# A dilated attention stage: permutation in smaller pieces, output weights loaded ahead of their split, one merge placed later

## The chip, the core and the metric

The kernel runs on one core of a Trainium2 chip. A core has a matrix engine (TensorE, in the profile PE, with its weight loads as PEld), a vector engine (VectorE, DVE), an activation engine (ScalarE, ACT), a general engine (GpSimd, POOL) and a queue engine that mostly issues transfers (SyncE, SP). Each takes its instructions in a fixed order and waits on semaphores for the others. The metric is the device time of one execution in microseconds, as the median over runs.

## The reference

Two encoder layers over 1024 tokens of width 1024. Layer 0 mixes tokens with latent attention, layer 1 with dilated windows; each ends with a squared-ReLU MLP. The change touches layer 1's mixer alone. What it must compute, shortened:

```python
DIL_GROUPS = ((128, 1), (512, 4), (2048, 16))      # window, dilation

def dilated_mixer(h, pos, w_in, g_q, g_k, rel_bias, w_o):
    proj = (h @ w_in).reshape(B, S, 3, 3, 16, 64)
    for gi, (window, dilation) in enumerate(DIL_GROUPS):
        q = rms_norm(proj[:, :, gi, 0], g_q[gi])
        k = rms_norm(proj[:, :, gi, 1], g_k[gi])
        v = proj[:, :, gi, 2]
        o, lse = dilated_group(q, k, v, pos, table, window, dilation)
        ...
    wts = jax.nn.softmax(jnp.stack(lses, axis=0), axis=0)
    o = jnp.einsum('gbsh,gbshd->bshd', wts, o_all)
    return o.reshape(B, S, 1024) @ w_o
```

So three groups of 16 heads attend, each over tokens taken at stride 1, 4 or 16, and their outputs are merged with weights from the three softmax denominators before the output projection.

## The kernel before

**Form of the numbers.** The program first runs a variant in which a matrix is a pair of 16-bit floats (a high and a low part), so that a product is three matmuls (`mm3`, L530 to L534). A second variant of the same code (`half` false) stands behind a branch, and the execution profiled here does not enter it. To split a loaded f32 weight into its pair takes one ACT instruction (L156, the high part) and one on DVE (L161, the low part).

**Order of the work.** The Python code gives an order, and a scheduler then moves instructions on each engine as far as their dependences allow; for PE the order of this stage is fixed as the code has it (`pin_from`). So where a step of the code lands on ACT, DVE, POOL and SP is seen in the built program.

**The dilated stage** is `dil` (L2194). It walks 96 steps `("qk", g, pr, tp)`: three groups g, eight pairs of heads pr, four blocks tp of 256 tokens; six steps without a projection follow. In one step the kernel

- scores two units of tokens of an earlier step on PE (`pss`, L2386), takes maxima and sums on DVE (`pd`, L2407, into `stat`), exponentiates on ACT (L2411, L2413), splits the result (`ph`, ACT L2450, DVE or POOL L2451) and transposes it with a DMA that SP issues (`pT`, L2452); in the last group's last pair PE transposes instead (`pspt`, L2439);
- projects 256 tokens to q and k on PE (`psproj`, L532 to L534, in two halves `project(..., 0, ...)` and `project(..., 1, ...)`);
- between those halves transposes q and k of an earlier step on PE (`psq`, L2354) and splits them into `kT` (ACT L2359, DVE L2360); the next scores read `kT`;
- multiplies by v on PE (`psav`, L2466 to L2468), which DVE copies to `U` (L2472, L2475);
- normalises the new q and k: squares on ACT (`dsq`, L2333), sum on DVE (`dms`, L2334), inverse root on ACT and DVE (`drl`, `dry`, `drt`: L132 to L136), product on DVE (`qn`, L2343) and gain on POOL or DVE (L2345).

Weights of q and k come pair by pair: `wqkr` is loaded by SP (L1968) and split to `wqk` (L156, L161).

**The permutation.** Groups 1 and 2 need the tokens in another order. `permute(g, dp, k)` (L2655 to L2684) copies one quarter of the channels of one part into new tiles `hTp` of the shared pool `G`; a call makes 4 copies of 128x512 for group 1 (`hTp<-hT` and `hTp<-hs`) and 8 of 128x256 for group 2 (`hTp<-hTp`). Copies go round by number over ACT (L2680), DVE (L2682) and POOL (L2684), two, two and one of five. There are eight calls before each new group: one at step (7, 2) of the old group, two at (7, 3), and five in `both` (L2232), which is the first projection of the new group, taken channel quarter by channel quarter. That first step is called the turn here.

**The merge.** `factors` (L2542 to L2558) makes the weights `mgf` of the three groups; `merge` (L2560 to L2569) multiplies group 2's `U` on DVE and the other groups' tiles `um` on POOL (L2567), and adds on DVE (L2569). It is called at a pair's last unit (`finish`). `emit` (L2576) transposes the merged pair on PE (`psot`, L2586) and splits it into `oT`, stored to memory for pairs 0 to 5 and kept for 6 and 7.

**The end of the stage.** `tail` (L2901) is called in the four last steps. It loads a quarter of the output weights (`wo_raw`, L1374, tile `wor`, L538 on SP) in the first and second of them, splits one (`wo_form`, tile `wo`) in the third and fourth, and in the fourth also loads and splits the other two (`wo_load`). Then `proj_res` (L1389) forms the output projection `psy`.

Of the kernel before, what the change touches and what calls it, by code (L numbers as in the profile page):

```python
# [15 lines left out]
ALU = mybir.AluOpType  # L16
# [4 lines left out]
P = 128  # L21
# [20 lines left out]
class K:  # L42
# [2151 lines left out]
    def dil(self, at0, at1, tail, wqk, vd, back=None):  # L2194
# [305 lines left out]
        O = [[[None] * 4 for _ in range(2)] for _ in range(2)]  # L2500
        merged = []

        def finish(u):
# [22 lines left out]
            if pr == 0:  # L2526
                sums_back(1)
            if pr < 7:
                f = factors(pr, 0, 8)
                for hf in range(2):  # L2530
                    merge(u, hf, f[:, :, 4 * hf : 4 * hf + 4])
                merged.append((u, u["at"], (0, 1)))
            else:
                last(u, 1)
# [41 lines left out]
        def emit(u, ths):  # L2576

            pr = u["pr"]
            if pr == 6:
                for k in range(2):  # L2580
                    for th in range(2):
                        O[k][th][3] = self.G(f"oT{k}", (P, 2, 512), self.DT)
# [72 lines left out]
        def permute(g, dp, k):  # L2655

            for th in range(2):
                if not self.half:
                    x = self.G("hTp", (P, 2, 512))
                elif k == 0:  # L2660
                    x = self.pair(self.G, "hTp", (P, 2, 512))
                    new_lo[(dp, th)] = x[1]
                    x = x[0]
                else:
                    x = new_lo.pop((dp, th))
# [30 lines left out]
        for n, step in enumerate(steps):  # L2696
            for f in vtodo.pop(n, ()):
                f()
            turn = step is not None and step[2:] == (0, 0) and bool(perms)
            if step is not None and step[1] < 2 and step[2] == 7 and step[3] >= 2:  # L2700
                if step[3] == 2:
# [15 lines left out]
            transposed, scored = scored, attend(ready, n > end) if ready else []  # L2717
            fetch(n)
            for u_, t_, _ in scored:
                if u_["g"] == 2:  # L2720
# [48 lines left out]
            if step is not None:  # L2769
                stacking = (u, tp, qkstep(u, tp, ps))  # L2770
                if n == end:
                    self.pin_from(mark, mybir.EngineType.PE)
# [3 lines left out]
                    if not self.half:  # L2776
                        for pp in range(3):
                            self.reload(O, src, pp, 0, nc.sync)
            if self.half and n == end + 1:
                back()  # L2780
# [19 lines left out]
def run(tc, a, half):  # L2800
    nc = tc.nc
    with ExitStack() as ctx:
# [97 lines left out]

        def tail(tp):  # L2901
            if tp < 2:
                raws.append(k.wo_raw(a["dil_w_o"][0], 0, tp))
# [76 lines left out]
```

## Time and profile before

| | us |
|---|---|
| median of 3 runs | 2974.12 (2973.5 to 2976.3) |
| the profiled execution, its own time | 2971.93 |
| its span, first to last instruction | 2970.1 |
| PE busy in the span | 2813.5 |
| DVE busy | 2237.1 |
| ACT busy | 1687.8 |

The mean granted clock of PE is 0.981. The dilated stage lies from about 1537 to 2275 us of the span, a step every 7.1 us; the turn to group 1 is near 1744 us, that to group 2 near 1982 us. A row of a timeline has the start, the duration, the engine, the line, the operation, the tiles written and read, the number of instructions, and in brackets how long the engine had been idle before and what released it. `x10` behind a row are ten instructions in a run. "Busy" of PE includes time at a lower clock.

### The profile page before, as it was taken

How to read it: one execution, taken by the hardware profiler on the slowest of the kernel's cores; microseconds unless marked ns; L12 is line 12 of the kernel's file. 1: busy time of each engine (PE TensorE's matmuls, PEld its weight loads, DVE VectorE, ACT ScalarE, POOL GpSimd, SP SyncE). 2: the span in 40 equal slices, each digit the busy share in tenths (PEclk: the TensorE clock that was granted, in tenths of full speed). 3: DMA queues.
4: the chain of work that ended last, by engine and by line, in shares of the span. 5: the costliest groups of instructions: out<-in, count | busy, mean ns of one | idle time of the engine just before them, and what ended most of it. 6: DMA issues, size and time to landing. Idle time of an engine off the chain costs nothing. (4 is left out here: it accounts for less than half of the span.)

```text
span 2970.1 us, 55695 instructions
## 1 busy us (share of the span) xinstructions
PE 2813.5 (95%) x20788; PEld 1678.5 (57%) x20788; DVE 2237.1 (75%) x4827; ACT 1687.8 (57%) x3491; POOL 924.9 (31%) x1272
## 2 busy tenths in 40 slices
PE   6888999999999999999999999998997999999998
PEld 5644566644444444443468888877875544444443
DVE  5687777648988866689757877777786698779565
ACT  4677888826455533452228878776664355555331
POOL 5578888700111000001113334445562001110010
PEclk9999999999999999999999999999998999999999
DMA  6267555424755689555635656756677555447753
GB/s 210 65 172 157 109 105 115 126 78 157 244 205 185 233 248 317 186 188 189 222 111 145 150 140 155 167 136 139 138 134 177 161 205 199 159 177 249 243 192 86
DMA packets 589684, 503.15 MB, mean 169 GB/s; under 512 B 292277, under 2 KB 482018, under 8 KB 589402
## 3 DMA queue, kind: packets, MB, share of 16 engines
q1 hardware_dynamic: 553722, 400.74, 48.9%
q0 software_dynamic: 25248, 87.22, 7.9%
q10 hardware_dynamic: 10432, 11.54, 1.7%
q8 instruction: 164, 2.69, 0.4%
q14 instruction: 118, 0.97, 0.1%
HBM read 317.40 MB, written 125.12 MB: 149 GB/s over the span
## 5 line engine op out<-in xcount | busy, mean ns | idle before, releaser
L532 PE MATMUL psm<-hf,wf 128*128 128x512 f16 x896 | 341.2, 381 | 5.1 <-ACT wf L156 5.1
L533 PE MATMUL psm<-d,d 128*128 128x512 f16 x896 | 340.4, 380 | 4.7 <-DVE d L161 4.7
L534 PE MATMUL psm<-hf,wf 128*128 128x512 f16 x896 | 335.0, 380 | 6.4 <-DVE wf L161 6.3
L533 PE MATMUL psm<-hf,wf 128*128 128x512 f16 x896 | 340.9, 380 | 0.0
L534 PE MATMUL psm<-d,d 128*128 128x512 f16 x896 | 340.4, 380 | 0.0
L532 PE MATMUL psm<-d,d 128*128 128x512 f16 x896 | 334.7, 380 | 0.3 <-ACT d L156 0.3
L1276 POOL TENSOR_TENSOR pp<-p,pp 128x1024 f16<-128x1024 f32 x125 | 275.5, 2209 | 57.9 <-ACT pp L1269 46.1
L532 PE MATMUL psproj<-wqk,hTp 128*128 128x256 f16 x1024 | 284.0, 277 | 0.0
L533 PE MATMUL psproj<-wqk,hTp 128*128 128x256 f16 x1024 | 283.5, 277 | 0.0
L534 PE MATMUL psproj<-wqk,hTp 128*128 128x256 f16 x1024 | 283.2, 277 | 0.0
L156 ACT ACTIVATE d<-ufr 128x1024 f16<-128x1024 f32 x112 | 117.8, 1052 | 211.9 <-PE psm L534 170.7
L897 DVE TENSOR_REDUCE mx<-pmx 128x1 f32<-128x512 f32 x240 | 162.9, 687 | 78.9 <-PE pmx L895 77.6
L161 DVE SCALAR_TENSOR_TENSOR d<-ufr,d 128x1024 f16<-128x1024 f32 x112 | 136.5, 1218 | 74.8 <-ACT d L156 74.7
L1268 ACT ACTIVATE p<-pss 128x512 f32<-128x512 f32 x256 | 150.1, 591 | 43.1 <-PE pss L1259 41.7
L2413 ACT ACTIVATE pd<-pd,dnb 128x192 f32<-128x192 f32 (+2 forms) x384 | 167.6, 438 | 2.6 <-ACT dnb L2411 0.4
L534 PEld LDWEIGHTS <-wf 128*128 128x128 f16 x896 | 87.8, 98 | 117.3 <-DVE wf L161 12.9
L532 PEld LDWEIGHTS <-wf 128*128 128x128 f16 x896 | 87.9, 98 | 112.7 <-ACT wf L156 9.6
L534 PEld LDWEIGHTS <-d 128*128 128x128 f16 x896 | 87.8, 98 | 110.8 <-issue 6.1
L271 DVE SCALAR_TENSOR_TENSOR adacc<-adaw,cond,adacc 128x1024 f32<-128x1024 f32 (+1 forms) x98 | 129.0, 1317 | 27.6 <-DMA adaw<-in_ada_w 26.7
L2451 POOL TENSOR_TENSOR ph<-pd,ph 128x512 f16<-128x512 f32 (+1 forms) x121 | 116.9, 970 | 104.0 <-ACT ph L2450 103.3
L532 PEld LDWEIGHTS <-d 128*128 128x128 f16 x896 | 87.9, 98 | 106.2 <-issue 2.0
L533 PEld LDWEIGHTS <-d 128*128 128x128 f16 x896 | 87.9, 98 | 106.1 <-issue 2.0
(445 smaller groups left out, 8176.9 us busy)
## 6 DMA issues: line engine op xcount, KB each, us to landing
ufr<-uf SPq DMA_DIRECT2D x112, 512.0 KB
w2r<-in_mlp_w SPq DMA_DIRECT2D x96, 512.0 KB
adaw<-in_ada_w SPq DMA_DIRECT2D x80, 512.0 KB
w1r<-in_mlp_w SPq DMA_DIRECT2D x64, 512.0 KB
wqkr<-in_dil_w_in SPq DMA_DIRECT2D x96, 256.0 KB
wvr<-in_dil_w_in SPq DMA_DIRECT2D x34, 512.0 KB
uf<-ub POOLq DMA_DIRECT2D x32, 512.0 KB, 3.7
uf<-ua POOLq DMA_DIRECT2D x32, 512.0 KB, 3.4
```

What stands on the lines that cost most here:

```text
L156: nc.scalar.activation(hi, src, AF.Copy, scale=scale)
L161: return nc.vector.scalar_tensor_tensor(lo, src, scale, hi, op0=ALU.mult, op1=ALU.subtract, accum_out=self.seen[:, self.nseen - 1 : self.n ...
L271: return self.nc.vector.scalar_tensor_tensor(acc, w, c, acc, op0=ALU.mult, op1=ALU.add)
L532: mm(out, lh, rh, start=first, stop=False)
L533: mm(out, lh, rl, start=False, stop=False)
L534: mm(out, ll, rh, start=False, stop=last)
L897: nc.vector.tensor_reduce(maxes[h][:, 2 * j + b : 2 * j + b + 1], ps, op=ALU.max, axis=AX.X)
L1268: nc.scalar.activation(p[:, b * 512 : (b + 1) * 512], ps[b], AF.Exp, scale=1.0 / self.ss)
L1276: eng.tensor_tensor(q[:, 1], p, q[:, 0], op=ALU.subtract)
L2413: nc.scalar.activation(p[:, e, lo:hi], p[:, e, lo:hi], AF.Exp, scale=1.0 / self.ss, bias=nb[:, e : e + 1], accum_out=stat[:, g, t, 1, 2 * ...
L2451: (nc.gpsimd if i or u["g"] == 2 else nc.vector).tensor_tensor(lo, p, hi, op=ALU.subtract)
```

## The change

Three things change, all of them in the variant with 16-bit pairs. In the code's order:

1. `permute` is called once in each of six steps, from (6, 2) on to (7, 3) of the old group, and the last two calls stay in `both`. Four of group 1's new tile pairs come from the stage's own pool rather than from `G`.
2. `tail` loads a quarter of the output weights in each of the last four steps and splits it two steps later; the last two splits fall behind the last projection.
3. The merge of pair 6, the last but one, is cut into pieces: `own` (U times its weight, DVE), `other` (a tile `um` times its weight, POOL), `add` (DVE) and `done`, spread over the three steps behind the last projection. It is emitted with the last pair.

```diff
+            if self.half and pr in (6,):
+                f = factors(pr, 0, 8)
...
+                if pr == 6:
+                    at, plan = end + 1, [[(other, 0, 1), (own, 0), (own, 1), (other, 0, 0)],
+                                         [(add, 0, 1), (add, 0, 0), (done, 0), (other, 1, 1), (other, 1, 0)],
+                                         [(add, 1, 1), (add, 1, 0), (done, 1)]]
...
-            if pr == 6:
+            if pr >= 6 and O[0][0][3] is None:
...
-                    x = self.pair(self.G, "hTp", (P, 2, 512))
+                    x = self.pair((lambda name, shape, dt: D_(f"h{dp}{th}", shape, dt, 1)) if g == 1 and dp < 2 else self.G, "hTp", (P, 2, 512))
...
-            turn = step is not None and step[2:] == (0, 0) and bool(perms)
-            if step is not None and step[1] < 2 and step[2] == 7 and step[3] >= 2:
+            turn = step is not None and step[1] > 0 and step[2:] == (0, 0)
+            if self.half and step is not None and step[1] < 2 and (step[2], step[3]) >= (6, 2):
+                if step[2:] == (6, 2):
+                    new = [[[], []], [[], []]]
+                    perms = [(step[1] + 1, dp, k) for dp in range(4) for k in range(2)]
+                for _ in range(1):
+                    if perms:
+                        permute(*perms.pop(0))
...
+            for f, *x in spread.pop(n, ()):
+                f(*x)
...
+            if self.half and n in (end + 1, end + 2):
+                tail(3 + n - end)
...
         def tail(tp):
+            if half:
+                if tp < 4:
+                    raws.append(k.wo_raw(a["dil_w_o"][0], 0, tp))
+                if tp > 1:
+                    wo[0].append(k.wo_form(raws.pop(0)))
+                return
```

In the changed kernel the copies of `permute` are L2708 (ACT), L2710 (DVE) and L2712 (POOL), `own` is L2533, `other` L2537, `add` L2541, the merge's weights L2579 to L2585.

**Where the scheduler puts it.** Of group 1's 32 copies, 16 (names `h_31...`, 7 on ACT, 6 on DVE, 3 on POOL) now stand at the very start of the dilated stage, ahead of its first square, and 16 stay at the turn. Of group 2's 64, 32 (13 on ACT, 13 on DVE, 6 on POOL) stand in one bunch, four to five steps ahead of the other 32, which stay at the turn. Two splits of `wqk` stand in that bunch too. The place of the bunch on DVE, in pair 6 of group 1, before: `kT_23608` is what the scores of the next unit wait for.

```order
L134 SCALAR_TENSOR_TENSOR drt_24328<-dms_24323,dry_24326 128x8
L135 SCALAR_TENSOR_TENSOR drt_24328<-drt_24328,dry_24326 128x8
L136 SCALAR_TENSOR_TENSOR dry_24326<-drt_24328,dry_24326 128x8
L2343 TENSOR_TENSOR qn_24338<-psproj_24237,dry_24326 128x512
L2451 TENSOR_TENSOR ph_24358<-pd_24360,ph_24358 128x512
L2360 SCALAR_TENSOR_TENSOR kT_23608<-psq_24408,kT_23608 128x2x256
```

And after; five more copies (`hTp_24487` and `hTp_24492`) stand in the rows just ahead of these, between L134 and L136.

```order
L2343 TENSOR_TENSOR qn_24338<-psproj_24237,dry_24326 128x512
L2710 COPY hTp_24790<-h_3163_20078 128x2x128
L2710 COPY hTp_24790<-h_3164_20081 128x2x128
L2710 COPY hTp_24795<-h_3163_20078 128x2x128
L2710 COPY hTp_24790<-h_3163_20078 128x2x128
L2710 COPY hTp_24790<-h_3164_20081 128x2x128
L2710 COPY hTp_24795<-h_3163_20078 128x2x128
L2710 COPY hTp_24795<-h_3164_20081 128x2x128
L161 SCALAR_TENSOR_TENSOR wqk_24497,seen_14494<-wqkr_24089,wqk_24497 128x1024
L2472 COPY U_23609<-psav_24439 128x256
L2451 TENSOR_TENSOR ph_24358<-pd_24360,ph_24358 128x512
L2360 SCALAR_TENSOR_TENSOR kT_23608<-psq_24408,kT_23608 128x2x256
```

Twelve copies, with one more a little ahead, and the split of a weight now stand before the `kT` of this step, which stood two rows behind `qn` before.

On ACT, at the end of the stage, in the third and fourth of the last steps; `wo` is a quarter of the output weights being split, `wor` its load. Before:

```order
L156 ACTIVATE wo_29917<-wor_29655 128x1024
L2411 ACTIVATE dnb_29709<-stat,ln_16275 128x2
L2413 ACTIVATE pd_29706,stat<-pd_29706,dnb_29709 128x128 x2
L2411 ACTIVATE dnb_29718<-stat,ln_16275 128x2
L132 ACTIVATE drl_29676<-dms_29672,misc 128x8
L156 ACTIVATE wo_29922<-wor_29920 128x1024
L2450 ACTIVATE ph_29704<-pd_29706 128x256
L2413 ACTIVATE pd_29715,stat<-pd_29715,dnb_29718 128x128 x2
L133 ACTIVATE dry_29675<-drl_29676 128x8
L2359 ACTIVATE kT_29416<-psq_29756 128x2x256
L2553 ACTIVATE mgf_29946<-mgf_29946 128x48
L2450 ACTIVATE ph_29704<-pd_29715 128x256
```

After:

```order
L156 ACTIVATE wo_29921<-wor_29655 128x1024
L2411 ACTIVATE dnb_29709<-stat,ln_16275 128x2
L2413 ACTIVATE pd_29706,stat<-pd_29706,dnb_29709 128x128 x2
L2411 ACTIVATE dnb_29718<-stat,ln_16275 128x2
L132 ACTIVATE drl_29676<-dms_29672,misc 128x8
L2450 ACTIVATE ph_29704<-pd_29706 128x256
L2413 ACTIVATE pd_29715,stat<-pd_29715,dnb_29718 128x128 x2
L133 ACTIVATE dry_29675<-drl_29676 128x8
L2359 ACTIVATE kT_29416<-psq_29756 128x2x256
L2581 ACTIVATE mgf_29940<-mgf_29940 128x48
L2450 ACTIVATE ph_29704<-pd_29715 128x256
L2333 ACTIVATE dsq_29806<-psproj_29731 128x512
```

The split of the third quarter, `wo_29922`, is gone from between the weights of the inverse root and `kT`; the fourth's, which came next after these rows before, is gone too. Both, on DVE as well, come behind the last but one `kT` of the stage or later.

On DVE, the last steps of the projection: the last `qn` (L2343, the last row) is what the last transposes and scores wait for; `um` are the other groups' tiles of pair 6. Before:

```order
L136 SCALAR_TENSOR_TENSOR dry_29808<-drt_29810,dry_29808 128x8
L2567 TENSOR_TENSOR U_28859<-U_28859,mgf_29946 128x512
L2343 TENSOR_TENSOR qn_29820<-psproj_29731,dry_29808 128x512
L2334 TENSOR_REDUCE dms_29966<-dsq_29965 128x8
L2569 TENSOR_TENSOR U_28859<-U_28859,um_29728 128x512
L2345 TENSOR_TENSOR qn_29820<-qn_29820,dgain 128x2x128
L2569 TENSOR_TENSOR U_28859<-U_28859,um_29728 128x512
L134 SCALAR_TENSOR_TENSOR drt_29971<-dms_29966,dry_29969 128x8
L135 SCALAR_TENSOR_TENSOR drt_29971<-drt_29971,dry_29969 128x8
L136 SCALAR_TENSOR_TENSOR dry_29969<-drt_29971,dry_29969 128x8
L2343 TENSOR_TENSOR qn_29981<-psproj_29861,dry_29969 128x512
```

After:

```order
L2334 TENSOR_REDUCE dms_29950<-dsq_29949 128x8
L2533 TENSOR_TENSOR U_28859<-U_28859,mgf_29940 128x512
L2541 TENSOR_TENSOR U_28859<-U_28859,um_29728 128x512
L134 SCALAR_TENSOR_TENSOR drt_29955<-dms_29950,dry_29953 128x8
L2541 TENSOR_TENSOR U_28859<-U_28859,um_29728 128x512
L135 SCALAR_TENSOR_TENSOR drt_29955<-drt_29955,dry_29953 128x8
L136 SCALAR_TENSOR_TENSOR dry_29953<-drt_29955,dry_29953 128x8
L2343 TENSOR_TENSOR qn_29965<-psproj_29863,dry_29953 128x512
```

All four adds of pair 6 still stand ahead of the last `qn`; the multiplication of the second half by its weight (L2567 before, L2533 now) does too, now behind the last `dms`. On POOL the four multiplications of `um` stay together, at the same place. On PE pair 6's eight transposes `psot` move from before the first `psy` to after its first products. On SP three loads of output weights, rather than two, stand ahead of the transposing DMA `pT_29579`, and none behind it.

More of the change, by code (lines that the diff above doesn't have):

```diff
@@ L2500, in dil @@
         O = [[[None] * 4 for _ in range(2)] for _ in range(2)]
-        merged = []
+        merged, spread, now = [], {}, [0]
         def finish(u):
@@ L2527, in finish, with own, other, add @@
                 sums_back(1)
-            if pr < 7:
+            if self.half and pr in (6,):
+                f = factors(pr, 0, 8)
+                def own(hf):
+                    U4 = u["U"][:, 4 * hf : 4 * hf + 4, :].rearrange("p t (h e) -> p t h e", h=2)
+                    nc.vector.tensor_tensor(U4, U4, f[:, 2, 4 * hf : 4 * hf + 4].unsqueeze(3).broadcast_to([P, 4, 2, 64]), op=ALU.mult)
+                def other(hf, k):
+                    x4 = u["um"][hf][:, :, k].rearrange("p t (h e) -> p t h e", h=2)
+                    nc.gpsimd.tensor_tensor(x4, x4, f[:, k, 4 * hf : 4 * hf + 4].unsqueeze(3).broadcast_to([P, 4, 2, 64]), op=ALU.mult)
+                def add(hf, k):
+                    U = u["U"][:, 4 * hf : 4 * hf + 4, :]
+                    nc.vector.tensor_tensor(U, U, u["um"][hf][:, :, k], op=ALU.add)
+                def done(hf):
+                    merged.append((u, now[0], (hf,)))
+                if pr == 6:
+                    at, plan = end + 1, [[(other, 0, 1), (own, 0), (own, 1), (other, 0, 0)],
+                                         [(add, 0, 1), (add, 0, 0), (done, 0), (other, 1, 1), (other, 1, 0)],
+                                         [(add, 1, 1), (add, 1, 0), (done, 1)]]
+                else:
+                    at, plan = now[0], [[(other, 0, 1), (own, 0)], [(other, 0, 0), (add, 0, 1)],
+                                        [(other, 1, 1), (add, 0, 0), (own, 1), (done, 0)],
+                                        [(other, 1, 0), (add, 1, 1)], [(add, 1, 0), (done, 1)]]
+                for i, fs in enumerate(plan):
+                    spread.setdefault(at + i, []).extend(fs)
+            elif pr < 7:
                 f = factors(pr, 0, 8)
@@ L2698, in dil @@
                 f()
-            turn = step is not None and step[2:] == (0, 0) and bool(perms)
-            if step is not None and step[1] < 2 and step[2] == 7 and step[3] >= 2:
+            turn = step is not None and step[1] > 0 and step[2:] == (0, 0)
[6 more added lines that the diff above has]
+                        permute(*perms.pop(0))
+            elif not self.half and step is not None and step[1] < 2 and step[2] == 7 and step[3] >= 2:
                 if step[3] == 2:
@@ L2718, in dil @@
             fetch(n)
+            now[0] = n
             for u_, t_, _ in scored:
@@ L2770, in dil @@
                 stacking = (u, tp, qkstep(u, tp, ps))
+            for f, *x in spread.pop(n, ()):
+                f(*x)
+            if step is not None:
                 if n == end:
```

## The prediction

> **What bounds the kernel now.** I read the page first, then PE's waits in the dilated stage, then the timelines around the places that the change touches.
>
> ```profile
> PE 2813.5 (95%) x20788; PEld 1678.5 (57%) x20788; DVE 2237.1 (75%) x4827; ACT 1687.8 (57%) x3491; POOL 924.9 (31%) x1272
> ```
>
> PE is busy 95% of the span, and the change alters none of its products. It can pay only where PE stands idle or runs at a lower clock. PE's waits from 1540 to 2320 us (us in total, times, longest):
>
> ```profile
> PE pss L2386 <- DVE kT L2360: 19.9, 13, 5.8
> PE psav L2466 <- DMA pT<-ph: 10.7, 6, 2.6
> PE pss L2386 <- DVE qn L2343: 7.1, 1, 7.1
> ```
>
> These are 37.7 us in all, of which the change reaches three places: the two turns and the stage's end. The waits of group 2 in between belong to merges of earlier pairs, which stay as they are.
>
> Turn 2 on PE's timeline, and in windows of 5 us (PE, PEld, DVE, ACT and POOL busy, then PE's granted clock):
>
> ```profile
> 1982.68 0.26 PE L2386 MATMUL pss<-kT 64*128 64x192 f16 x2 [1.17 <-ACT kT L2359]
> 1988.77 0.50 PE L2386 MATMUL pss<-kT 64*128 64x192 f16 x4 [5.83 <-DVE kT L2360]
> ...
> 1980.00:1985.00 5.00, 1.77 (x37) 1.30 (x34) 5.00 (x10) 5.00 (x14) 4.18 (x8) 1.00 1.12 221
> 1985.00:1990.00 5.00, 1.23 (x8) 0.72 (x9) 4.70 (x19) 4.70 (x13) 1.04 (x4) 0.54 0.59 124
> 1990.00:1995.00 5.00, 5.00 (x38) 4.12 (x36) 2.79 (x10) 2.82 (x11) 0.00 (x0) 0.78 0.34 77
> ```
>
> PE stands 1.17 + 5.83 = 7.0 us here. Then the granted clock is 0.54 and 0.78 where it is 1.00 elsewhere: in the last window PE works 5.00 us and 0.22 of that is lost, 1.1 us; with the 1.23 us worked at about half clock just before, some 0.6 more, the half-clock stretch costs 1.7 us.
>
> **Turn 1** (one term). Its waits on PE:
>
> ```profile
> 1745.01 0.61 PE L2386 MATMUL pss<-kT 64*128 64x256 f16 x8 [0.82 <-DVE kT L2360]
> 1752.78 0.20 PE L2466 MATMUL psav<-vs,pT 128*128 128x64 f16 x1 [1.37 <-DMA pT<-ph]
> 1754.46 0.34 PE L2386 MATMUL pss<-kT 64*128 64x192 f16 x4 [0.38 <-DVE kT L2360]
> 1758.73 0.44 PE L2354 MATMUL psq<-ident,qn 128*128 128x128 f32 x2 [1.20 <-DVE qn L2343]
> ```
>
> They sum to 3.8 us. The order puts 16 of the 32 copies at the start of the stage: 7 on ACT, 6 on DVE, 3 on POOL. What hides them there:
>
> ```profile
> 1539.52 0.60 ACT L2333 ACTIVATE dsq<-psproj 128x512 f32<-128x512 f32 x1 [34.62 <-PE psproj L534]
> 1541.67 0.36 DVE L2209 SCALAR_TENSOR_TENSOR dgain<-dgain,dgk 128x192 f32<-128x192 f32 x1 [4.86 <-DMA dgk<-in_dil_g_k]
> ...
> L2680 ACT ACTIVATE hTp<-hT x10: 639/662/674, 1736.5 to 1750.3; 128x512 f16<-128x512 f16 x10
> L2682 DVE COPY hTp<-hT x10: 410/460/906, 1737.7 to 1749.9; 128x512 f16<-128x512 f16 x10
> ```
>
> ACT needs 7 x 0.66 = 4.6 us of an idle 34.62; DVE 6 x 0.46 = 2.8 of 4.86; POOL's three stand ahead of one of its stores of v, which is read a step or more later. I cost them at nothing; without that cover DVE's 2.8 us would be the price. At the turn DVE keeps 7 of 13 copies. The waits on DVE there, 0.82 + 0.38 + 1.20 = 2.4, mostly go; the transposing DMA's 1.37 has its own chain and stays. I take **-2.2**, between 0 (the 7 copies left still come before a `kT`) and -3.8 (all of it).
>
> **Turn 2 and the new bunch** (two terms). The DVE copies of group 2, and how they lie at the turn:
>
> ```profile
> L2682 DVE COPY hTp<-hTp x25: 273/484/1231, 1976.7 to 1988.8; 128x256 f16<-128x256 f16 x25
> ...
> 1977.50 5.06 DVE L2682 COPY hTp<-hTp 128x256 f16<-128x256 f16 x12
> 1982.48 1.21 DVE L161 SCALAR_TENSOR_TENSOR wqk<-wqkr,wqk 128x1024 f16<-128x1024 f32 x1
> 1983.63 3.55 DVE L2682 COPY hTp<-hTp 128x256 f16<-128x256 f16 x10
> 1988.04 0.67 DVE L2360 SCALAR_TENSOR_TENSOR kT<-psq,kT 128x512 f16<-128x512 f32 x1
> ```
>
> The runs of 12 and 10 take (5.06 + 3.55) / 22 = 0.39 us a copy. 23 copies stood ahead of that `kT`. Now 12 do: 11 x 0.39 = 4.3 us earlier, so PE's 7.0 shrinks to 2.7. Whether the half-clock stretch (1.7) then goes is open; I take half of it, 0.8. Turn 2 gives **-5.1** (bounds -4.3, and -8.7 for all of it).
>
> The other 13 DVE copies, `U` and the split of a weight come ahead of a `kT` in pair 6. That place before:
>
> ```profile
> 1950.60 0.69 DVE L2451 TENSOR_TENSOR ph<-pd,ph 128x512 f16<-128x512 f32 x1 [1.43 <-ACT ph L2450]
> 1951.21 0.68 DVE L2360 SCALAR_TENSOR_TENSOR kT<-psq,kT 128x512 f16<-128x512 f32 x1
> 1952.76 0.67 PE L2386 MATMUL pss<-kT 64*128 64x192 f16 x12
> 1953.47 0.41 DVE L2472 COPY U<-psav 128x256 f32<-128x256 f32 x1
> ```
>
> `kT` ends at 1951.89 and the scores begin at 1952.76: the chain has 0.87 us to spare, and DVE idled 1.43 before. Added ahead of `kT`: 13 x 0.39, the split's 1.15 (1983.63 - 1982.48) and 0.41, together 6.6 us, less 1.43 and 0.87: PE stands 4.3 us. Counted from turn 2 instead, which is left with one copy less and already had `U` there, it is 2.7 + 0.39 + 0.41 = 3.5. I take 4.0 and, as before, half of a half-clock stretch: **+4.8**. The lower bound is 2.8, with copies at the shortest 0.273; the upper 4.8 + 1.7 = 6.5, with copies at the 5.06 / 12 = 0.42 of the run that POOL's copies stand beside.
>
> A gain is excluded, since nothing is taken away there. The `qn` behind the bunch is not late: PE takes it a step (7.1 us) later.
>
> What the clock does is seen at two places: the stretch behind the 5.83 us above, and this one at the end of the stage, where PE works 3.89 us at a granted 0.50, some 1.9 lost, though the longest of the waits ahead of it (quoted next) is 2.56:
>
> ```profile
> 2250.00:2255.00 5.00, 3.89 (x26) 2.60 (x27) 4.93 (x18) 2.36 (x6) 1.51 (x5) 0.50 0.54 57
> ```
>
> By that row a wait of 2.7 at turn 2 and one of 4.0 in the bunch may each bring a stretch: turn 2 -4.3, bunch +5.7. The Trainium skill ("TensorE: Matmul & The Clock Gate", HAM oscillation) allows idle gaps of up to about 3.4 us without a fall of the clock. By that rule turn 2 would be -6.0 and the bunch +5.7, and the sum below -6.7 rather than the -5.0 that the row gives; the row at 2250 speaks against the rule. My halves lie between what the two say of each place.
>
> **The end of the stage** (one term). On PE, and what it waits for:
>
> ```profile
> 2248.39 0.23 PE L2466 MATMUL psav<-vs,pT 128*128 128x64 f16 x1 [2.56 <-DMA pT<-ph]
> 2250.25 0.29 PE L2386 MATMUL pss<-kT 64*128 64x128 f16 x2 [1.04 <-ACT kT L2359]
> 2251.40 0.72 PE L2386 MATMUL pss<-kT 64*128 64x128 f16 x10 [0.86 <-DVE kT L2360]
> 2266.93 0.82 PE L2386 MATMUL pss<-kT 64*128 64x128 f16 x11 [7.06 <-DVE qn L2343]
> 2274.80 0.38 PE L2386 MATMUL pss<-kT 64*128 64x128 f16 x4 [1.32 <-DVE oT L161]
> ...
> 2247.48 1.06 ACT L156 ACTIVATE wo<-wor 128x1024 f16<-128x1024 f32 x1 [4.17 <-DMA wor<-in_dil_w_o]
> 2252.68 1.21 DVE L161 SCALAR_TENSOR_TENSOR wo<-wor,wo 128x1024 f16<-128x1024 f32 x1
> 2255.87 0.21 DVE L2557 TENSOR_TENSOR mgf<-mgf,mgd 128x48 f32<-128x48 f32 x1
> 2256.16 5.53 POOL L2567 TENSOR_TENSOR um<-um,mgf 128x512 f32<-128x512 f32 x4 [4.07 <-DVE mgf L2557]
> 2266.18 0.69 DVE L2343 TENSOR_TENSOR qn<-psproj,dry 128x512 f32<-128x512 f32 x1
> ```
>
> ACT waits 4.17 us for a load that it has to split, and `kT` and `ph` queue behind it. With the splits moved back, ACT's `kT` is ready when `psav` ends, so the waits of 1.04 and 0.86 go. DVE loses two splits of 1.21 ahead of `mgf`, and `mgf` comes at about 2252.2 instead of 2255.87: 1.04 + 0.86 earlier scores, plus the second split and part of the first. POOL's 5.53 us of `um` begin with it. The four adds still stand ahead of the last `qn`, so the last `qn` keeps hanging on POOL's `um`: it moves 3.7 us, not the whole 7.06. Behind it the 1.32 for `oT` goes, as pair 6's transposes stand later; they covered a wait for the last `kT` (a pass on ACT and one on DVE, each about the 0.67 of the DVE row above, 1.3, of which I leave 0.5 covered by the products that stay), so 0.8 comes back. Their own time is moved, not saved. The two late splits lie beside `psy`, on engines that wait there. Sum: -3.7 - 1.3 + 0.8 = **-4.2**; bounds -7 (the low clock of 2250 to 2255 goes as well, 1.9, and the 0.8 doesn't come) and 0 (something else holds the last `qn`).
>
> **Sum:** -2.2 - 5.1 + 4.8 - 4.2 = -6.7. The profiled execution took 2971.93 us (span 2970.1 and 1.8 around it), so 2965.2. It lies 2.2 below the median of the runs shown; against that, 2967.4, say **2967**.
>
> **Rivals.**
>
> *More goes than I count* (2960.5): turn 1 -3.4, turn 2 -6.0 with no slow clock left, bunch +2.8, end -7: -13.6. For it speaks that turn 1's waits of up to 1.37 are followed by none; against it that `kT` has only 0.87 us to spare. Chance 0.30.
>
> *Not what it says* (2972.7): the permutation isn't spread over six steps but falls in bunches, as the order shows, so group 2's wait is only moved. Turn 1 -0.6, turn 2 -4.3, bunch +6.5, end -3: -1.4. Chance 0.16.
>
> *Slower, by a load in SP's queue.* SP issues in order, and a third load of weights now stands ahead of the transposing DMA whose `psav` waited 2.56 us:
>
> ```profile
> 2232.38 6.96 SPq L538 DMA_DIRECT2D wor<-in_dil_w_o x2
> 2241.76 1.24 SPq L2452 DMA_TRANSPOSE pT<-ph  x1
> 2238.98 8.48 DMA wor<-in_dil_w_o
> ```
>
> SP was free at 2239.34, 2.4 us before it issued that transposition. If the third load must wait for the landing of one before it, up to 6.96 + 8.48 = 15.4 us, `pT` comes 13.0 late; 3.7 of that is won back behind it. Turns -2.5, end +9.3, clock +1.7: +8.5, 2982.6. It ends slower from a wait of about 12.8 us; below 2.4 it costs nothing. Against it: the loads go to buffers of their own, and the first two were issued in 6.96 together. Chance 0.12.
>
> **Numbers.** The forecast's own case has 0.42, from 2963 to 2971; about a third of it (0.14) lies within 0.2% of 2974.12 (2968.2 to 2980.1, about what a measurement of this kernel can tell from no change). So faster 0.30 + 0.28 = 0.58, same 0.16 + 0.14 = 0.30, slower 0.12. The range reaches from 2956, below the gain of the first rival, to 2978; what lies beyond is most of the slower case and the edge of the first.
>
> **What would show it.** Right: sixteen copies before 1540 with no new wait on PE; a wait of 3 to 4 us for `kT` near 1953, and one of about 2.7 near 1982 where 7.0 stood; ACT's wait for `wor` gone near 2247; the wait for the last `qn` at 5 us or so, with POOL's `um` beginning near 2252. Wrong: no wait near 1953; a wait of `psav` above 2.56 near 2246 with SP held at a `wor`; the last `qn` no earlier against the last projection than now.

## The result, and the profile after

The changed kernel is slower: 2984.1 us in the median of seven executions (2978.99 to 2989.28) against 2976.12 for the kernel before (eight, 2973.5 to 2980.55). The ratio is 1.0028, 95% interval 1.0018 to 1.0037, so +8.3 us (5.4 to 11.0). One further execution, 4743.98 us at a mean granted clock of 0.614, was disturbed and is left out. The forecast was 2967 (2956 to 2978), a gain of 7. The profiled execution after took 2982.83 us (span 2981.0), 10.9 more than the one before.

The page's first line shows that the work is the same; only its time differs.

```profile
PE 2819.1 (95%) x20788; PEld 1678.9 (56%) x20788; DVE 2239.3 (75%) x4827; ACT 1686.9 (57%) x3491; POOL 922.2 (31%) x1272
```

PE's waits from 1540 to 2330 us, after (us in total, times, longest):

```profile
PE pss L2386 <- DVE kT L2360: 17.2, 16, 3.4
PE psav L2466 <- DMA pT<-ph: 13.3, 7, 5.3
PE psot L2614 <- DVE U L2597: 6.6, 3, 3.8
PE pss L2386 <- ACT kT L2359: 5.0, 3, 3.0
PE pss L2386 <- DVE qn L2343: 4.4, 1, 4.4
```

The waits on DVE's `kT` and on its `qn` have shrunk by 2.7 us in total each, as meant. What stands against that are ACT's `kT` (one wait of 3.0) and the transposing DMA (longest 5.3 for 2.6). `psot` has one wait more than before, of 2.6 us near 2306.

**Where the time went.** PE issues 20,788 products in both kernels, nearly all in the same order, so the start of the product of the same number in both traces gives the delay at each point of the program. What each stretch adds to the delay (us; place in the time of before; the last four columns belong to the experiments):

```
stretch                         forecast   after |  e1 perm.  e2 weights  e3 merge  e4 early half
turn 1         1722 to 1766       -2.2     -1.5  |   -1.5       -0.1        0.0      +0.6
               1766 to 1940                +1.1  |   +0.4       +0.8       +2.1      +0.6
new bunch      1940 to 1974       +4.8     +4.5  |   +4.9        0.0        0.0      +3.0
turn 2         1974 to 2006       -5.1     -1.0  |   -0.5       +0.2       +1.3      -0.7
               2006 to 2221                +1.1  |   -1.2       +0.7       +1.6      +1.2
               2221 to 2245                -1.7  |   -1.7       -1.7       -0.1       0.0
end of stage   2245 to 2335       -4.2     +4.3  |   +0.3       -0.2       +3.2      -3.7
behind it      2335 to 2959                +0.4  |    0.0        0.0       +0.4      +3.7
```

From 1722 us on this is +7.2 for the changed kernel. Of the other 3.7 us between the two profiled executions, 3.3 arose ahead of the stage, in code that no edit touches, and 0.4 behind PE's last product. The other kernels below lie between -1.6 and +4.8 ahead of the stage, so this is the spread of single executions. The rows between the named places come and go with a stretch of half clock near 1790 and one near 2225, and e4's +0.6 at turn 1 holds a stretch from 1756.7 to 1760.2; the last section shows why.

**Turn 2.** On PE's timeline, and in windows of 5 us (PE, PEld, DVE, ACT and POOL busy, PE's granted clock):

```profile
1991.99 0.26 PE L2386 MATMUL pss<-kT 64*128 64x192 f16 x2 [2.96 <-ACT kT L2359]
1995.01 0.50 PE L2386 MATMUL pss<-kT 64*128 64x192 f16 x4 [2.77 <-DVE kT L2360]
...
1990.00:1995.00 5.00, 0.26 (x2) 0.10 (x2) 4.99 (x12) 4.96 (x12) 3.26 (x5) 0.73 0.98 193
1995.00:2000.00 5.00, 4.99 (x30) 3.56 (x31) 3.91 (x15) 4.12 (x17) 1.33 (x4) 0.59 0.48 110
```

PE stands 2.96 + 2.77 = 5.7 us where it stood 7.0, and the half clock behind it is still there. The wait on DVE fell from 5.83 to 2.77, very near the 2.7 that the forecast gave, but the wait on ACT just ahead of it grew from 1.17 to 2.96. Before and after, on DVE and ACT, from the timelines of the turn; first before:

```profile
1974.11 0.69 DVE L2334 TENSOR_REDUCE dms<-dsq 128x8 f32<-128x512 f32 x1 [1.03 <-ACT dsq L2333]
1974.84 0.30 ACT L132 ACTIVATE drl<-dms,misc 128x8 f32<-128x8 f32 x1 [0.82 <-DVE dms L2334]
1978.29 1.08 ACT L2680 ACTIVATE hTp<-hTp 128x256 f16<-128x256 f16 x3
```

and after:

```profile
1980.50 0.69 DVE L2451 TENSOR_TENSOR ph<-pd,ph 128x512 f16<-128x512 f32 x1 [2.23 <-ACT ph L2450]
1984.17 0.68 DVE L2334 TENSOR_REDUCE dms<-dsq 128x8 f32<-128x512 f32 x1
1984.88 0.30 ACT L132 ACTIVATE drl<-dms,misc 128x8 f32<-128x8 f32 x1 [2.83 <-DVE dms L2334]
1987.07 2.57 DVE L2710 COPY hTp<-hTp 128x256 f16<-128x256 f16 x6
1987.94 1.09 ACT L2708 ACTIVATE hTp<-hTp 128x256 f16<-128x256 f16 x3
1991.30 1.50 DVE L2710 COPY hTp<-hTp 128x256 f16<-128x256 f16 x6
```

DVE's twelve copies take 4.07 us for the 8.61 of 22, so the saving was counted rightly: 4.5 us. But the last reduction ahead of them, `dms`, comes 10.06 us later than before, while PE is 7.4 late there: DVE did `ph` of the step before at 1980.50 only, and `kT`, `dry`, `qn` and `U` of that step stand between. ACT, which needs `dms`, waits 2.83 for it instead of 0.82 and comes to its copies 9.65 us later than before; DVE comes to its own 9.57 later. So both come to the turn about 2.2 us behind PE. From DVE's first copy to the start of its `kT` the saving is 3.3 us rather than 4.5 (7.21 for 10.54), as DVE waits 0.37 there for ACT's split of `wqk`, and that split's part on DVE and `ph` take longer (1.36 for 1.21, 1.30 for 0.67). What is left, 3.3 - 2.2 = 1.1, is about the 1.0 that PE gained.

The lateness begins at the bunch. Set against PE, DVE's `dms` starts within 0.4 us of where it did before in the three steps up to 1946 us of before. In the step of the bunch it is 5.6 us late, and 3.3, 3.7 and 2.7 in the next three, the last of which is the row above. It is not a backlog of work, since DVE idles 2.23 us ahead of that `ph`: from the bunch on, the built order has `dms`, `drt`, `dry` and `qn` later in the step.

**The new bunch**, in pair 6 of group 1, on PE, DVE and ACT:

```profile
1952.90 2.73 DVE L2710 COPY hTp<-h 128x256 f16<-128x256 f16 x7
1955.55 1.21 DVE L161 SCALAR_TENSOR_TENSOR wqk<-wqkr,wqk 128x1024 f16<-128x1024 f32 x1
1957.18 0.26 PE L2386 MATMUL pss<-kT 64*128 64x192 f16 x2 [1.16 <-ACT kT L2359]
1957.63 0.68 DVE L2360 SCALAR_TENSOR_TENSOR kT<-psq,kT 128x512 f16<-128x512 f32 x1
1958.37 0.50 PE L2386 MATMUL pss<-kT 64*128 64x192 f16 x4 [0.93 <-DVE kT L2360]
```

The copies run ahead of `kT`, as the order said. PE's two waits come to 2.1 us; against the kernel before it then loses 1.4 to a half clock up to 1961.7, and the rest of the 4.5 in steps of 0.2 to 0.3 us up to 1974.

**Turn 1.** The copies at the stage's start cost PE nothing, and at the turn one wait is left (1.66 us for `pT`, at 1757). But the order had also moved a split of `wqk` two steps ahead of the turn, and ACT waits for its load; `kT` queues behind it:

```profile
1718.64 1.06 ACT L156 ACTIVATE wqk<-wqkr 128x1024 f16<-128x1024 f32 x1 [1.35 <-DMA wqkr<-in_dil_w_in]
1726.71 0.26 PE L2386 MATMUL pss<-kT 64*128 64x192 f16 x2 [0.88 <-ACT kT L2359]
1727.44 0.34 PE L2386 MATMUL pss<-kT 64*128 64x192 f16 x4 [0.47 <-DVE kT L2360]
```

**The end of the stage.** PE's waits, one by one, after:

```profile
2256.89 0.23 PE L2466 MATMUL psav<-vs,pT 128*128 128x64 f16 x1 [5.32 <-DMA pT<-ph]
2270.73 0.83 PE L2386 MATMUL pss<-kT 64*128 64x128 f16 x12 [4.43 <-DVE qn L2343]
...
2306.57 1.12 PE L2614 MATMUL psot<-ident,U 128*128 128x128 f32 x4 [2.61 <-DVE U L2597]
2309.31 2.29 PE L532 MATMUL psy<-wo,oT 128*128 128x512 f16 x5 [1.63 <-ACT wo L156]
```

Up to 2296 us of before the stage's end gains: the waits of 1.04 and 0.86 for `kT` and of 1.32 for `oT` are gone and the last `qn` waits 4.43 for 7.06, while `psav` waits 5.32 for 2.56. Net, PE's delay falls from 5.7 to 3.9 us. The long wait of `psav` also holds the merge, since on DVE the copy of `psav` stands ahead of the merge's weights:

```profile
2257.75 0.42 DVE L2472 COPY U<-psav 128x256 f32<-128x256 f32 x1 [4.30 <-PE psav L2468]
2259.97 0.21 DVE L2585 TENSOR_TENSOR mgf<-mgf,mgd 128x48 f32<-128x48 f32 x1
```

`mgf` comes 4.1 us later than before (2255.87) where PE is 5.7 late, so only 1.6 earlier against PE, and POOL's `um` begin with it at 2260.25.

Then come the last two of PE's rows above. The last four products of `psot` stand ahead of all products of the second half of the output projection now, and PE waits for the merge that feeds them; and the splits of that half stand behind ACT's copy of that last `psot`. ACT, after:

```profile
2307.72 0.60 ACT L156 ACTIVATE oT<-psot 128x512 f16<-128x512 f32 x1 [6.93 <-PE psot L2614]
2308.21 3.88 ACT L156 ACTIVATE wo<-wor 128x1024 f16<-128x1024 f32 x4
```

and before:

```profile
2293.51 0.60 ACT L156 ACTIVATE oT<-psot 128x512 f16<-128x512 f32 x1 [3.42 <-PE psot L2586]
2294.00 0.59 ACT L2443 ACTIVATE pT<-pspt 128x512 f16<-128x512 f32 x1
2294.48 3.89 ACT L156 ACTIVATE wo<-wor 128x1024 f16<-128x1024 f32 x4
```

Before, the four splits ran at 2294.48, beside the first half's products, and PE had second-half products with which to bridge the last merge. After, ACT idles 6.93 us and splits from 2308.21 on, with PE waiting. The two gaps make 4.2 us, and the half clock behind them costs the rest:

```profile
2305.00:2310.00 5.00, 1.80 (x6) 1.07 (x7) 3.09 (x7) 2.28 (x3) 0.00 (x0) 0.63 1.04 249
2310.00:2315.00 5.00, 5.00 (x17) 1.93 (x16) 5.00 (x10) 2.10 (x3) 0.00 (x0) 0.69 1.04 234
```

In the second window 31% of the 5.00 us is lost. From 2296 to 2335 us of before, the delay rises by 6.1.

### The profile page after: what moved, and what is told of

Read it like the earlier page. It is cut to its first block, busy times and chain, and to the rows that moved or that the text cites. A ratio compares the mean times of both kernels' runs of the same rounds, so it can differ in the third digit from the quotient of the medians.

```text
span 2981.0 us, 55693 instructions
## 1 busy us (share of the span) xinstructions
PE 2819.1 (95%) x20788; PEld 1678.9 (56%) x20788; DVE 2239.3 (75%) x4827; ACT 1686.9 (57%) x3491; POOL 922.2 (31%) x1272
## 3 DMA queue, kind: packets, MB, share of 16 engines
q8 instruction: 164, 2.69, 0.4%
## 5 line engine op out<-in xcount | busy, mean ns | idle before, releaser
L532 PE MATMUL psproj<-wqk,hTp 128*128 128x256 f16 x768 | 213.3, 278 | 0.0
L533 PE MATMUL psproj<-wqk,hTp 128*128 128x256 f16 x768 | 212.7, 277 | 0.0
L534 PE MATMUL psproj<-wqk,hTp 128*128 128x256 f16 x768 | 212.4, 277 | 0.0
L534 PEld LDWEIGHTS <-wf 128*128 128x128 f16 x896 | 87.8, 98 | 119.8 <-DVE wf L161 15.9
L532 PEld LDWEIGHTS <-wf 128*128 128x128 f16 x896 | 87.9, 98 | 112.4 <-ACT wf L156 9.6
L533 PEld LDWEIGHTS <-wf 128*128 128x128 f16 x896 | 88.0, 98 | 105.2 <-issue 1.6
```

The lines of the kernel that those rows point to most:

```text
L532: mm(out, lh, rh, start=first, stop=False)
L533: mm(out, lh, rl, start=False, stop=False)
L534: mm(out, ll, rh, start=False, stop=last)
```

## The experiments

After the result the question was which part costs what. The theory was that the merge behind the last projection costs most, by the last `psot` and the splits behind it (A in the first expectations); the rivals were that the permutation, above all its new bunch, is the whole loss (B), and that the three loads ahead of the transposing DMA are (C). All ratios are against the kernel before, 11 or 12 executions against 21 to 35. A part "alone" is the changed kernel with the other two parts as before.

**The permutation alone** (e1).

```diff
-            if self.half and pr in (6,):
+            if self.half and pr in (9,):
...
-            if self.half and n in (end + 1, end + 2):
-                tail(3 + n - end)
...
-            if half:
-                if tp < 4:
...
-                return
```

> Only part 1 of the change (the permutation in six steps). Theory A (the loss lies at the end of the stage, in the last pair's transposes that now stand ahead of the second half of the output products): the traces of the two kernels differ by 2.9 us on PE between the stage's start and 2226 us, so this kernel is about 3 us slower than before, with the end of the stage as before. Theory B (the permutation is the loss: the bunch, a weight's split that waits for its load, more time at half clock): the whole 8 us, ratio 1.0028.

Measured: 1.0008 (0.9999 to 1.0017), +2.4 us. The waits at turn 2 are those of the changed kernel (view of PE's waits, 1975 to 2000 us):

```profile
PE pss L2386 <- ACT kT L2359: 2.9, 1, 2.9
PE pss L2386 <- DVE kT L2360: 2.7, 1, 2.7
```

So turn 2's lost gain and the bunch belong to the permutation and to nothing else, and together with turn 1 they make +2.8 on the trace, as A has it. It is not the whole loss. At the end of the stage, with the output weights as before, `psav` waits 4.85 us here for 2.56, and the two waits for `kT` behind it are gone: that wait can grow without the second part.

**The weights alone** (e2): the changed kernel with the third part's `pr in (6,)` as above and the permutation as before.

```diff
-                    x = self.pair((lambda name, shape, dt: D_(f"h{dp}{th}", shape, dt, 1)) if g == 1 and dp < 2 else self.G, "hTp", (P, 2, 512))
+                    x = self.pair(self.G, "hTp", (P, 2, 512))
...
-            if self.half and step is not None and step[1] < 2 and (step[2], step[3]) >= (6, 2):
+            if self.half and step is not None and step[1] < 2 and False:
...
-            elif not self.half and step is not None and step[1] < 2 and step[2] == 7 and step[3] >= 2:
+            elif step is not None and step[1] < 2 and step[2] == 7 and step[3] >= 2:
```

> Only part 2 (output weights loaded ahead of their split). Theories A and B: 1 to 3 us faster than before, as the waits of 1.04 and 0.86 for kT go, and a wait of psav for its transposing DMA takes back up to 2.8 (5.32 instead of 2.56). Theory C (the third load ahead of that DMA in SP's queue is the loss): 3 us slower or more.

Measured: 0.9997 (0.9988 to 1.0006). No loss, so the loads ahead of the transposing DMA are not the loss, as C would have it. But of the 1 to 3 us that A and B forecast, little is seen either. `psav` waits 4.86 us for 2.56 and the last `qn` 4.13 for 7.06, with `kT`'s two waits gone; from 2246 to 2300 us PE's waits are 11.2 us for 14.5. The half clock there takes back what is won: it lasts 20.5 us (2249.9 to 2256.7 and 2263.5 to 2277.2) for 17.1 before, and PE now works 15.2 us of it rather than standing, for 8.3 before. At a granted 0.50 that is 3.4 us more lost.

**The merge alone** (e3): both edits above, `pr in (6,)` kept.

> Only part 3 (pair 6's merge behind the last projection). Theory A: the wait for the last transposes (2.6 us), the wait for the splits of the second half of the output weights (1.6) and the half clock behind them (2.4) are all here: about 5 us slower than before, since a little is won ahead of it. Theory B: no difference, within 1 us.

Measured: 1.0006 (0.9997 to 1.0015), +1.8 us by the ratio, less than A's 5. On the trace the end of the stage costs +3.2: the splits again stand behind the last `psot`, which here waits 0.52 us only, and PE waits 1.63 for `wo`:

```profile
2301.10 0.66 PE L2614 MATMUL psot<-ident,U 128*128 128x128 f32 x4 [0.52 <-DVE oT L161]
...
2309.76 0.58 PE L532 MATMUL psy<-wo,oT 128*128 128x512 f16 x1 [1.63 <-ACT wo L156]
```

**The changed kernel with the second half's weights loaded earlier** (e4). The raw loads of the second half go to the last `tail`, so its splits and two thirds of a row of its products come to stand ahead of the last `psot` again.

```diff
+                if tp == 5:
+                    raws.extend(k.wo_raw(a["dil_w_o"][0], 1, dp) for dp in range(4))
...
-        wo[1] = [k.wo_load(a["dil_w_o"][0], 1, dp, k.X) for dp in range(4)]
+        wo[1] = [k.wo_form(raws.pop(0), k.X) if half else k.wo_load(a["dil_w_o"][0], 1, dp, k.X) for dp in range(4)]
```

> The changed kernel whole, and the second half of the output weights loaded as soon as the last quarter of the first half is split, so that the order has their four splits, and two thirds of a row of products, ahead of the last pair's last transposes. Theory A: the waits of 2.6 and 1.6 us and the half clock at 2306 go, 5 to 7 us faster than the changed kernel, 2978 to 2980, about 3 us slower than before. Theory B: as the changed kernel, 8 us slower than before.

Measured: 1.0014 (1.0005 to 1.0023), half of the loss of the changed kernel. PE's waits from 2272 to 2335 us are down to this:

```profile
PE pspt L2439 <- ACT pd L2413: 1.7, 1, 1.7
PE psy L532 <- ACT oT L156: 0.2, 1, 0.2
PE pss L2386 <- DVE kT L2360: 0.2, 1, 0.2
```

From 2221 to 2335 us the kernel gains 3.8 where the changed kernel loses 2.6: 6.4 us better, and the forecast's -4.2 for the end nearly comes in. So the order of the last `psot` and the splits is what the end of the stage lost by. But in the MLP that follows, +3.7 is given back, most of it from 2390 to 2440 us, where the waits for the splits of its own weights, `wf`, come to 5.6 us (3.3 before).

Up to 2305 us this kernel's order on PE, DVE, ACT and POOL is the changed kernel's, so the two show how the half clock near 2225 and the wait behind it go together. Here that stretch stays as before, `psav` waits 3.73, and PE gains 3.3 from 2245 to 2296; in the changed kernel the stretch is absent (-1.7), `psav` waits 5.32 and the gain is 1.8. From 2221 to 2296 both gain about 3.4.

**The permutation for one turn only** (e5: group 1; e6: group 2), with the other two parts as before.

```diff
-            if self.half and step is not None and step[1] < 2 and (step[2], step[3]) >= (6, 2):
+            if self.half and step is not None and step[1] == 0 and (step[2], step[3]) >= (6, 2):
```

> Part 1 for the first turn only (16 of 32 copies at the start of the stage), the rest as before. Theory A (each turn is what its own trace rows show): PE 1.5 us earlier behind the first turn, no wait in pair 6 of group 1, turn 2 as before (1.17 and 5.83): 1 to 2 us faster. Theory B (the copies at the stage's start or the split ahead of its load cost more than the turn gains): 1 us slower or more.

> Part 1 for the second turn only. Theory A: the bunch in pair 6 of group 1 costs PE 4.6 us, two waits of about 1 us and a half clock behind them, and turn 2 gives back only 0.5 to 1: 4 us slower. Theory B (the bunch is harmless by itself and only late because the first turn ran differently): within 1 us of before.

Measured: e5 0.9998 (0.9988 to 1.0007), which decides between neither of its theories; e6 (`step[1] == 1`) 1.0008 (0.9999 to 1.0016), +2.4 us. Turn 1 alone gives -1.5 on the trace, as in the changed kernel. Turn 2 alone has the bunch at +3.0 (its waits the same 1.2 + 0.9, but no half clock) and -0.9 at the turn (waits 2.9 + 2.8). So the small gain at turn 2 has nothing to do with what was done to group 1.

**Turn 2 without the bunch** (e7). None of the three parts; instead 32 of group 2's 64 copies are made straight from the original order of the tokens, at the start of the stage, into four pairs of tiles of their own, and the turn keeps the other 32.

```diff
+        def permute_far(dp, k):
...
+                    src = self.raw(HT[oh][k][dp])
+                    i_ = src.rearrange("p d (l a r) -> p d a r l", a=4, r=4)
+                    o_ = x.rearrange("p d (a r l) -> p d a r l", a=2, r=4)
...
+            if self.half and n == 0:
+                for dp in (0, 1):
+                    for k in range(2):
+                        permute_far(dp, k)
```

> None of the three parts; half of group 2's copies are instead made from the tokens in their first order, into four tiles of the stage's own, so that they are ready at the start of the stage. Theory A (turn 2's wait is what stands on DVE ahead of kT, and in the changed kernel the bunch left DVE and ACT late): no bunch, PE's 7.0 us at turn 2 fall to about 2.7, and with luck the half clock goes: 4 to 6 us faster. Theory D (half the copies leave the wait at turn 2 as it is, as in the changed kernel: 5.7 us): 1 us faster at most.

Measured: 2972.01 us, 0.9985 (0.9976 to 0.9993): 4.5 us faster than the kernel before and faster than the changed one. Turn 2 gives -4.7, close to the forecast's -5.1; PE's waits from 1975 to 2000 us:

```profile
PE pss L2386 <- DVE kT L2360: 1.6, 1, 1.6
PE pss L2386 <- ACT kT L2359: 0.8, 1, 0.8
```

The copies are not quite free at the start: +2.4 up to 1663 us, a wait of 0.91 for the first `qn` at 1547.66 among it. Half the copies off the turn are thus worth what was forecast when the steps ahead of it are left alone: up to the turn `dms`, `qn` and `kT` stand in time against PE as in the kernel before, where the changed kernel's `dms` is 2.7 to 5.6 us late. But these copies also read another tile, and the order at the turn itself differs a little, so that the bunch is what made the difference is supported, not proven.

**The same with the end of the stage** (e8: e7 with parts two and three and the edit of e4), **with the 32 copies on ACT alone** (e9), and **e9 with the second part** (e10).

```diff
-                        put(o_[:, :, q, :, 32 * oh : 32 * oh + 32], i_[:, :, 2 * th + q])
+                        nc.scalar.activation(o_[:, :, q, :, 32 * oh : 32 * oh + 32], i_[:, :, 2 * th + q], AF.Copy)
```

> The copies as in the run named for far copies at the start, with parts 2 and 3 and the second half of the output weights loaded early. Theory A: 4 to 6 us from the second turn and 2 to 4 from the end of the stage, 6 to 10 us faster than before. Theory D: 2 to 4 us faster, all of it at the end.

> As the run with far copies at the start alone, but all 32 of these copies on ACT, which idles 22 to 34 us there. Theory A (in that run DVE's 13 copies made PE wait 0.9 us at 1547, and cost up to 1.7 there in all): turn 2 as in that run, no wait at 1547, 5 to 6 us faster than before. Theory E (a run's wait at the start is not from these copies): as that run, 4 us faster.

> The same and part 2 of the change. Theory A: the places are independent, so 1 to 2 us more at the end of the stage as on the trace of part 2 alone: 6 to 8 us faster than before. Rival: part 2 alone measured 1 us faster with an interval of 2.7 either way, so it may add nothing: 5 us.

Measured: e8 0.9992 (0.9983 to 1.0001), with -4.8 at turn 2 and -3.2 from 2245 to 2335 us, and +3.7 given back in the MLP as in e4. e9 0.9989 (0.9980 to 0.9998): the wait for the first `qn` stays (1.1 us), so it was not DVE's share of the copies that held it. e10 0.9991 (0.9982 to 1.0000). None is better than e7, and all three fell short of their first theory: 6 to 10, 5 to 6 and 6 to 8 us forecast, 2.4, 3.3 and 2.7 measured.

**Two parts at a time** (e11: weights and merge; e12: permutation and merge). The three parts alone add up to +3.3 us, not to 8.3. In the next two expectations A, B and C stand for: the parts add; weights and merge together cost more; the permutation and the merge together do.

> The second and third part together, permutation as before. Alone the parts measured 1.0008 (permutation), 0.9997 (weights) and 1.0006 (merge), which adds up to 1.0011, some 3 us, where the whole change measured 1.0028, 8.3 us. Theory A, parts add and the rest is spread between runs: 1.0003 (about +1 us); on the trace the end of the stage costs +3.1 - 1.9 = +1.2 us. Theory B, weights and merge together make a longer gap at the last transposes than the merge alone (2.6 us and then 1.6 in the changed kernel, 0.5 and 1.6 with the merge alone, and twice the stretch of half clock): 1.0010 to 1.0020 (+3 to +6 us), the end of the stage at +2.5 us or more on the trace, the gap of 2.6 back. Theory C, the rest comes from the permutation together with another part: 1.0003 here, as in A, and the next run carries it.

> The first and third part together, output weights loaded and split as before. Theory A, parts add: 1.0014 (+4 us); on the trace turn 1 -1.5, the bunch +4.5 to +4.9, turn 2 -0.5 to -1.0, the end of the stage about +3. Theory B, weights and merge make the rest: 1.0014 here as well. Theory C, the rest comes from the permutation together with the merge: 1.0020 or more (+6 us or more), and the trace shows at the end of the stage more than the +3.1 of the merge alone.

Measured: e11 1.0011 (1.0002 to 1.0020), e12 1.0018 (1.0009 to 1.0027). The gap at the last `psot` is back in e11, as B has it:

```profile
2303.12 1.12 PE L2614 MATMUL psot<-ident,U 128*128 128x128 f32 x4 [2.61 <-DVE U L2597]
2305.87 2.29 PE L532 MATMUL psy<-wo,oT 128*128 128x512 f16 x5 [1.63 <-ACT wo L156]
```

and the end of the stage costs +3.7 from 2245 to 2335 us. But the time is at the lower edge of B, and within the interval of A; C has +2.2 at the end in e12, less than the merge alone, and falls on the trace. Taken as three terms that add, the six ratios (e1, e2, e3, e11, e12 and the change) are fitted best by +3.4 us for the permutation, +0.7 for the weights and +2.7 for the merge, 6.7 in all, and none lies more than 1.6 us from that, where each has an interval of about 2.7 either way. So the parts may simply add; whether some 1.5 us of the 8.3 come from weights and merge together stays open. The traces put it lower: from 2221 to 2335 us the weights alone give -1.9, the merge alone +3.1 and both together +2.0, which is 0.8 more than their sum.

## Why the prediction was wrong, step by step

The four terms were -2.2, +4.8, -5.1 and -4.2, in sum -6.7; on the trace they are -1.5, +4.5, -1.0 and +4.3, in sum +6.3. Of the 13.0 us between the sums, 8.5 are the end of the stage and 4.1 are turn 2. Timed, the permutation alone is +2.4 where its three terms gave -2.5, and weights and merge together +3.3 where the fourth gave -4.2.

**The copies at the stage's start at nothing, turn 1 at -2.2:** right in kind. No wait arose at the start, and the turn gave 3.1 us. The 1.35 us that ACT waits for the load of a hoisted `wqk` was not seen, and the term came to -1.5.

**The bunch at +4.8:** the copies did hold `kT` and PE, as forecast, but the number (+4.5) is right by luck in part. The waits are 2.1, against 4.0; a half clock of 1.4, of which the forecast had booked half a stretch, and small steps make up the rest.

**Turn 2 at -5.1: failed.** The step was "23 copies stood ahead of that `kT`. Now 12 do: 11 x 0.39 = 4.3 us earlier". The copies were saved, 4.5 us of them. But the sum held fixed the time at which DVE and ACT begin the turn's copies against PE, and these began about 2.2 us later; 1.2 more went between the copies and `kT`. ACT's `kT`, a wait that the forecast did not treat apart, grew by 1.8. That the wait on DVE fell to 2.77, about the 2.7 forecast for both waits, is luck, since PE came to it later by what it had stood for ACT just ahead. What was left is -1.0. e6 shows that the permutation of group 2 alone does this; e7 that the term is -4.7 without the bunch.

**The end of the stage at -4.2: failed**, and this decided the sign. Up to 2296 us it went the forecast's way, though by 1.8 only: the waits for `kT` and `oT` went, the last `qn` waits 4.43 (forecast: 5 or so), but `psav` waits 5.32. ACT's wait of 4.17 for `wor` is gone: both splits there begin without a wait. "`mgf` comes at about 2252.2 instead of 2255.87", 3.7 us earlier, came to 1.6, since `mgf` queues on DVE behind a copy of the late `psav`; the last `qn` came 2.0 us earlier against PE. The transposition that `psav` waits for was issued at 2247.91, 6.15 us later than before where PE is 5.7 late, and SP was free from 2243.39 on, so the loads did not hold it. The product that reads it began 9.0 us behind the issue, against 6.6. That time is 6.6 to 9.0 us over all the kernels here, and 8.9 in e1, where the loads are as before. Why it is longer in some traces stays open.

The step that turned the gain into a loss is the next one: "Their own time is moved, not saved. The two late splits lie beside `psy`, on engines that wait there." It looked at the two late splits of the first half. The four splits of the second half, and its products, were moved behind the last `psot` by the edit of the merge, and cost 4.2 us of waits and 1.9 of clock. With the merge alone (e3) the splits stand there too, and the same stretch from 2296 to 2335 us costs 3.1; with the weights as well (e11) it is 6.1 again; e4 takes it away. With a gain of 4.2 there, and all else as measured, the change would have been faster by some 2 us.

**The rivals.** "Slower, by a load in SP's queue" ended on the right side by the wrong mechanism: the three loads were issued in 3.59 us, and e2 is not slower.

```profile
2239.80 3.59 SPq L538 DMA_DIRECT2D wor<-in_dil_w_o  x3
```

"Not what it says" had the nearest mechanism, that group 2's wait is only moved; bunch and turn 2 together are +3.5, where it gave +2.2.

**The clock.** The halves of a stretch that the forecast booked at turn 2 and in the bunch were guesses: at turn 2 the stretch stayed, and in the bunch it came (it did not in e6).

## What to carry to other kernels

When work is moved ahead of a stall, price the stall by when its engines will begin, not by what is taken off their list: work put a few steps earlier on the same in-order engines can shift the order of the steps between, and those engines then arrive late at the stall. And when the last piece of a stage is moved back, follow in the built order everything that the edit carries along on each engine up to the next stage's first products; here four weight splits that nobody edited went behind a late copy on ACT, and cost more than the edit could win. Copies that depend on nothing late can be made far ahead, where an engine idles for long, as at this stage's start; in e7 that gave 4.7 us at the turn and cost 2.4 at the start.

## What the runs showed of the hardware

**PE's clock is decided on a fixed grid.** In all fourteen traces here every change of the granted clock lies within 0.005 us of a grid of 3.413 us that runs through the whole execution, and with the grid most of the half clock can be read off. Counted over the fourteen traces, from the clock's first record on, all 217 of the grid's windows that ran at full clock with PE busy under 40% were followed by one at half clock; from 40 to 50% 36 of 92; from 50 to 65% 19 of 162; above that none of 11,121. So whether a wait of about 2 us brings a stretch depends on how it falls on the grid. In e11 and e12 PE waits the same 1.84 us at the same place:

```profile
2228.46 0.45 PE L2386 MATMUL pss<-kT 64*128 64x128 f16 x10 [1.84 <-DVE kT L2360]
```

```profile
2228.65 0.45 PE L2386 MATMUL pss<-kT 64*128 64x128 f16 x10 [1.84 <-DVE kT L2360]
```

In e11's windows of the grid (length, then the five engines' busy time, PE's first, then the granted clock) the idle time falls across two windows, PE is busy 2.30 and 2.69 us in them, and the clock stays:

```profile
2224.32:2227.73 3.41, 2.30 (x31) 1.94 (x28) 3.41 (x7) 1.79 (x6) 3.41 (x3) 1.00 0.02 7
2227.73:2231.15 3.42, 2.69 (x32) 2.35 (x32) 3.42 (x14) 1.07 (x4) 3.42 (x5) 1.00 0.00 0
2231.15:2234.56 3.41, 3.41 (x34) 3.12 (x32) 3.34 (x7) 2.67 (x12) 2.84 (x7) 1.00 0.34 77
```

In e12's it falls into one, PE is busy 1.57 us of it, and the next window runs at half clock, which costs 1.7 us:

```profile
2226.01:2229.42 3.41, 1.57 (x31) 1.22 (x30) 3.41 (x6) 0.60 (x1) 3.41 (x4) 0.99 0.00 0
2229.42:2232.83 3.41, 3.41 (x19) 2.43 (x17) 3.38 (x14) 2.56 (x12) 3.33 (x6) 0.51 0.06 14
```

The grid's position differs from execution to execution. So gaps that sum to about 2 us within 3.4 bring or do not bring a stretch by chance, 1.7 us each, and a single profile cannot price an edit at such a place closer than that. The Trainium skill ("TensorE: Matmul & The Clock Gate", What's actually happening) has this window of 3413 ns and that it runs free; the traces agree. The rule that the Trainium skill gives under the same title (HAM oscillation), no idle gaps beyond about 3.4 us, is too wide by these rows: 1.84 us were enough.

**A single execution's spread.** Code ahead of the stage that is the same in all these kernels differs by -1.6 to +4.8 us between their profiled executions and that of the kernel before. Medians agree better (the kernel before has 2975.12 to 2976.30 in five sets of 8 to 35 executions), and the terms above were read as steps in the delay within one trace, rather than as totals, for that reason.
